# The eight transposes of the attention's q move from the PSUM tags s and o to the PSUM tag c

## The chip, the cores and the metric

One core of one Trainium2 chip runs the kernel. The time is device microseconds of one execution. The kernel before took 844.49 us, the median of three runs (843.57 to 844.58 us). The core has five engines with a queue of instructions each: TensorE (PE in the profile, with its weight loads as PEld), VectorE (DVE), ScalarE (ACT), GpSimd (POOL) and SyncE (SP). Matrix products are written into PSUM, which the kernel uses as eight banks of 128 x 512 float32.

## The reference, cut to what matters

One layer of an encoder on 512 tokens of width 1024. Three sub-layers follow one another, each between two RMS norms and added to the residual: a token mixer, a cross-attention into 256 memory rows, and a gated MLP with a short convolution. The change lies in the mixer, whose input projection feeds two groups of heads:

```python
h = rmsnorm(x, pre_mix_g)
aq, ak, av, hq, hf_fwd, hf_bwd, hi, hg = split_columns(h @ w_in, IN_SPLITS)
aq = rmsnorm(aq.reshape(b, n, 8, 64), q_norm_g)
ak = rmsnorm(ak.reshape(b, n, 2, 64), k_norm_g)
att = axial_gqa_attention(apply_rope(aq, cos, sin), apply_rope(ak, cos, sin), av)
rec = hgrn2_group(hq, hf_fwd, hf_bwd, hi, hg, ...)      # four recurrent heads
mixed = concatenate([att, rec]) @ w_out
```

So q has 8 heads of 64 columns for 512 tokens. It is projected token by token, normalised and rotated, and then transposed, since the scores need q with its columns on the partitions.

## The kernel before, in words

**Precision.** A float32 product is made of three matmuls on a high and a low part (`mm3`, lines 149 to 151). A value is split into these parts by a cast on ACT (line 103) and a subtraction on DVE (line 104).

**PSUM.** A tile of a bank is taken with `bank(tag)`. There are four tags, b, s, o and c, with two banks each. Tag b serves the projections whose output has its columns on the partitions, s and o the projections in token order and later the scores (s) and the transposed probabilities and outputs (o) of the attention. Tag c serves the recurrent cores (`hgrn_core`), and `spread_r` once at the start.

**Order.** The program is written as generators that `weave` interleaves in the text of the program. The framework then places the instructions on each engine's queue ahead of the run: an earlier place in the program goes first among those that it holds ready, and a later one may be put ahead of an earlier one that still waits. Once placed, the order in a queue is fixed. A tile whose tag has no free buffer waits for the release of an older one.

**The stage of the change.** `mix_projections` (line 662) ends with the projection of q in token order and the three projections of the last recurrent head:

- `proj_tm` on line 670 computes q for four blocks of 128 tokens. Its four banks are `tm_tags`, s, s, o, o: blocks 0 and 1 stand in the two banks of s, blocks 2 and 3 in the two of o. What is to be done with a block (`put_qn`, line 629) is only noted in the list `late`.
- `hgrn_in(3, late)` on line 671 projects head 3's q and its two forget gates (called f0 and f1 below) into tag b, each followed by a `scaled` use (line 451, DVE) that reads the bank, then by sigmoids on ACT (lines 470, 477, 478) and products on DVE (471, 480). After the first projection it runs `put_qn` of blocks 0 and 1, after the second that of blocks 2 and 3.
- `put_qn` of a block calls `norm_rope`, which reads the block's bank three times: a square on ACT (line 593) and two products on DVE (602 and 605). With the sums (595), the inverse root on POOL (167, 168, 597), the addition (606) and the scaling (607) it makes the rotated rows, which are split (103, 104) into `qs`. Then two groups of four transposes (line 637) each fill one bank: the first four heads, copied by ACT into `qT[0]` (line 641), and the last four, copied by DVE into `qT[1]` (line 639). There are 32 transposes and eight copies in all.
- After that comes one weave of three streams: the recurrent core of head 3 (`hgrn_core(3)`, tag c, whose first product is line 506 and its copy line 507), the attention (line 704: scores on line 711 in tag s, softmax from line 689, transposes of the probabilities on line 721 in tag o, and the weighing of v on line 733), and a filler (line 769): projections of the memory (`proj_fm` with 256 columns, two banks of tag b in turn, called memory column blocks below), whose output is split by `put_kx` (lines 103 and 104 on `ps_b`), then the output projection of the mixer.

The scores of item i take one bank of s and read `qT` at token block i % 4 of head i // 4. The high and low parts of scores are two matmuls.

Of the kernel before, what the change touches and what calls it, by code (L numbers as in the profile page):

```python
# [73 lines left out]
def layer(tc, io, out):  # L74
# [15 lines left out]
    def bank(tag):  # L90
        return ps.tile([P, 512], F32, name="ps_" + tag, tag=tag)
# [7 lines left out]
    def tmp4(shape, dt=F32):  # L99
        return t4.tile(shape, dt, name="tmp4", tag="tmp4")  # L100

    def split(hi, lo, src, eng=None):
        nc.scalar.copy(hi, src)  # L103
        (eng or nc.vector).tensor_sub(lo, src, hi.bitcast(F32))  # L104
# [48 lines left out]
    def blk(b):  # L153
        return slice(b * P, (b + 1) * P)
# [434 lines left out]
    def norm_rope(z, nh, which, b):  # L589
        n = nh * 64  # L590
        rope = qkv["rope"]
        u = tmp2()
        nc.scalar.activation(u[:, :n], z, ACT.Square, scale=r[:, b:b + 1])
        ss = small()
        nc.vector.tensor_reduce(ss[:, :nh], u[:, :n].rearrange("p (h d) -> p h d", h=nh), axis=AX.X, op=ALU.add)
        rz = rstd_of(ss[:, :nh], nh, 64)
        nc.gpsimd.tensor_scalar(rz[:, :nh], rz[:, :nh], r[:, b:b + 1], 0.0, op0=ALU.mult, op1=ALU.add)
        xn = tmp2()
        x3 = xn[:, :n].rearrange("p (h d) -> p h d", h=nh)
        st = rope[:, 2 * which + 1, b, :]  # L600
        ss4 = st.rearrange("p (i two) -> p i two", two=2)[:, None].to_broadcast([P, nh, 32, 2])
        nc.vector.tensor_tensor(out=u[:, :n].rearrange("p (h i two) -> p h i two", h=nh, two=2),
                                in0=pat(z, 1, [[64, nh], [2, 32], [-1, 2]]), in1=ss4, op=ALU.mult)
        ct = rope[:, 2 * which, b, :][:, None, :].to_broadcast([P, nh, 64])
        nc.vector.tensor_tensor(out=x3, in0=z.rearrange("p (h d) -> p h d", h=nh), in1=ct, op=ALU.mult)
        nc.vector.tensor_add(xn[:, :n], xn[:, :n], u[:, :n])
        nc.vector.tensor_tensor(out=x3, in0=x3, in1=rz[:, :nh, None].to_broadcast([P, nh, 64]), op=ALU.mult)
        return x3
# [20 lines left out]
    def put_qn(b, z):  # L629
        qr = norm_rope(z, 8, 0, b)  # L630
        qs = tmp4([P, 8, 2, 64], F32R)
        split(qs[:, :, 0, :], qs[:, :, 1, :], qr)
        q3 = qs.rearrange("p h a d -> p h (a d)")
        for g in range(2):
            o = bank("so"[g]).rearrange("p (k n) -> p k n", k=4)
            for i in range(4):
                nc.tensor.transpose(o[:, i, :].bitcast(F32R), q3[:, 4 * g + i, :], ident_r)
            if g:
                nc.vector.tensor_copy(qkv["qT"][g][:, :, blk(b)], o)
            else:  # L640
                nc.scalar.copy(qkv["qT"][g][:, :, blk(b)], o)
# [20 lines left out]
    def mix_projections():  # L662
        yield from proj_tm(hT, tm_tags, put_sg)
        mem_norm()
        yield from hgrn_in(1)
        yield from hgrn_in(2)
        mem_turn()
        yield from proj_tm(hT, tm_tags, put_kv, 256)
        late = []
        yield from proj_tm(hT, tm_tags, lambda b, z: late.append(lambda: put_qn(b, z)))  # L670
        yield from hgrn_in(3, late)
# [351 lines left out]
```

## Time and profile before

| | |
|---|---|
| median of three runs | 844.49 us (843.57 to 844.58) |
| the profiled execution's own time | 846.16 us |
| its span in the trace | 844.3 us |
| PE busy in the span | 828.5 us (98%) |
| DVE busy | 488.2 us (58%) |
| ACT busy | 427.7 us (51%) |
| mean granted clock of PE | 0.996 |

The span runs from the first to the last instruction that the trace shows; the profiled execution is 1.86 us longer than it. PE is busy nearly all the time, so a change of this size has to be read from the short stretch in which it works: 186 to 218 us after the start of the span. In the timelines of the prediction each row has the start in us, the duration in us, the engine, the line and operation, the tile written and the tiles read, their shape, how many instructions were merged, and in brackets the idle time of the engine before it with what ended that. In the table of stretches, each engine has its busy time with its count of instructions, then come the granted clock of PE, the share of time that the DMA engines were busy, and GB/s.

### The profile page before, as it was taken

What the parts mean: (1) busy time and instruction counts of PE and PEld (TensorE: products, weight loads), DVE (VectorE), ACT (ScalarE), POOL (GpSimd) and SP (SyncE); (2) the same over time, 40 slices, a digit from 0 to 9 for tenths busy, and PEclk for the clock granted to TensorE, in tenths of its full rate; (3) what the DMA queues carried; (4) which work ended last, traced back from release to release, by engine and by line L of the source; (5) the groups of instructions that cost most, each with busy time, mean ns of one, the idle gap of its engine ahead of it and who ended that gap; (6) DMA issues with size and microseconds to landing.
All of it is one profiled execution on the core that took longest, in us unless ns stands there. A gap on an engine that the chain in (4) does not pass through costs nothing.

```text
span 844.3 us, 11078 instructions
## 1 busy us (share of the span) xinstructions
PE 828.5 (98%) x4304; PEld 703.4 (83%) x4304; DVE 488.2 (58%) x759; ACT 427.7 (51%) x736; POOL 102.4 (12%) x163
## 2 busy tenths in 40 slices
PE   9999999997999999999999999999999999999996
PEld 7888888886999888888888998888888888888885
DVE  5364677619996775854444865555555557722224
ACT  6576656546898874645443553333333335511121
POOL 0212202317223201300001300000000000000001
PEclk9999999999999999999999999999999999999999
DMA  9687754477477643341302333322222222322312
GB/s 322 182 202 203 159 112 113 101 153 181 98 157 162 149 131 119 101 160 65 125 25 75 99 126 101 101 95 88 93 99 99 100 101 94 101 88 94 99 50 100
DMA packets 29796, 101.81 MB, mean 121 GB/s; under 512 B 3952, under 2 KB 4464, under 8 KB 29744
## 3 DMA queue, kind: packets, MB, share of 16 engines
q1 hardware_dynamic: 22752, 77.38, 27.3%
q0 software_dynamic: 6272, 22.81, 14.7%
q10 hardware_dynamic: 720, 0.92, 0.3%
q8 instruction: 34, 0.56, 0.3%
q14 instruction: 18, 0.15, 0.1%
HBM read 99.00 MB, written 2.10 MB: 120 GB/s over the span
## 4 chain that ended last, share of the span: by engine, by line
PE 91%; DVE 3%; ACT 2%; DMA 2%; POOL 1%; issue 1%; POOLq 0%; DVEq 0%; ACTq 0%
PE ps_b L149 9%; PE ps_b L150 9%; PE ps_b L151 9%; PE ps_s L151 6%; PE ps_s L149 6%; PE ps_s L150 6%; PE ps_o L149 6%; PE ps_o L151 6%; PE ps_o L150 6%; PE ps_c L149 4%; PE ps_c L150 4%; PE ps_c L151 4%; PE ps_c L516 3%; PE ps_o L733 2%; PE ps_s L711 2%; PE ps_o L721 2%
## 5 line engine op out<-in xcount | busy, mean ns | idle before, releaser
L104 DVE TENSOR_TENSOR wl<-raw,wh 128x1024 fp32r<-128x1024 f32 x93 | 113.8, 1224 | 199.9 <-ACT wh L103 199.8
L103 ACT CAST wh<-raw 128x1024 fp32r<-128x1024 f32 x93 | 97.9, 1053 | 206.2 <-PE ps_o L151 71.4
L149 PE MATMUL ps_b<-big,wh 128*128 128x512 f32 (+1 forms) x320 | 118.6, 371 | 2.1 <-DVE tmp L451 2.1
L150 PE MATMUL ps_b<-big,wh 128*128 128x512 f32 (+1 forms) x320 | 117.5, 367 | 0.0
L151 PE MATMUL ps_b<-big,wl 128*128 128x512 f32 (+1 forms) x320 | 117.3, 367 | 0.0
L149 PEld LDWEIGHTS ps_b<-big,wh 128*128 128x128 f32 x320 | 61.0, 191 | 11.3 <-DVE tmp L451 2.3
L151 PEld LDWEIGHTS ps_b<-big,wl 128*128 128x128 f32 x320 | 60.9, 190 | 9.3
L150 PEld LDWEIGHTS ps_b<-big,wh 128*128 128x128 f32 x320 | 60.9, 190 | 9.0
L177 POOL TENSOR_SCALAR small<-small 128x1 f32<-128x1 f32 x40 | 13.9, 348 | 440.7 <-ACT tmp L208 421.8
L149 PE MATMUL ps_s<-wh,big 128*128 128x512 f32 (+1 forms) x140 | 54.1, 387 | 0.0
L151 PE MATMUL ps_s<-wh,big 128*128 128x512 f32 (+1 forms) x140 | 53.3, 381 | 0.0
L150 PE MATMUL ps_s<-wl,big 128*128 128x512 f32 (+1 forms) x140 | 53.0, 379 | 0.0
L542 DVE TENSOR_TENSOR big<-big 128x512 f32<-128x512 f32 x64 | 47.9, 755 | 8.4 <-PE ps_c L516 4.6
L126 ACT CAST wh<-raw 128x1024 fp32r<-128x1024 f32 x35 | 36.7, 1048 | 30.3 <-PE ps_o L151 16.1
L149 PE MATMUL ps_o<-wh,big 128*128 128x512 f32 (+1 forms) x124 | 47.9, 386 | 0.0
L151 PE MATMUL ps_o<-wh,big 128*128 128x512 f32 (+1 forms) x124 | 46.7, 377 | 0.0
L150 PE MATMUL ps_o<-wl,big 128*128 128x512 f32 (+1 forms) x124 | 46.7, 377 | 0.0
L131 POOL DMA_DIRECT2D wl<-in_w_dram x35 | 31.2, 892 | 112.9 <-ACT wl L128 103.3
L104 DVE TENSOR_TENSOR big<-ps_o,big 128x512 fp32r<-128x512 f32 x52 | 35.7, 688 | 15.1 <-ACT big L103 14.9
L103 ACT CAST big<-ps_o 128x512 fp32r<-128x512 f32 x52 | 30.3, 586 | 19.6 <-PE ps_o L830 7.5
L149 PE MATMUL ps_b<-wh,big 128*128 128x512 f32 x92 | 36.7, 399 | 0.0
L150 PE MATMUL ps_b<-wl,big 128*128 128x512 f32 x92 | 36.2, 393 | 0.0
(248 smaller groups left out, 1949.2 us busy)
## 6 DMA issues: line engine op xcount, KB each, us to landing
raw<-in_w_dram SPq DMA_DIRECT2D x131, 512.0 KB, 3.3
wl<-in_w_dram POOLq DMA_DIRECT2D x35, 512.0 KB, 5.6
big<-in_x_dram SPq DMA_DIRECT2D x8, 512.0 KB, 7.5
big<-in_xt_dram SPq DMA_DIRECT2D x3, 512.0 KB, 7.8
big<-in_mem_dram POOLq DMA_DIRECT2D x2, 512.0 KB, 8.2
out_dram<-big SPq DMA_DIRECT2D x4, 256.0 KB, 2.0
out_dram<-big ACTq DMA_DIRECT2D x3, 256.0 KB, 2.0
big<-in_xt_dram SPq DMA_DIRECT2D x2, 256.0 KB, 3.5
```

Of the source, the lines that this page charges most:

```text
L103: nc.scalar.copy(hi, src)
L104: (eng or nc.vector).tensor_sub(lo, src, hi.bitcast(F32))
L126: nc.scalar.copy(wh, raw)
L131: nc.gpsimd.dma_start(wl, io["w"][i], accum_op=ALU.add)
L149: nc.tensor.matmul(o, a[0], b[0], start=start, stop=False)
L150: nc.tensor.matmul(o, a[0], b[1], start=False, stop=False)
L151: last_mm[0] = nc.tensor.matmul(o, a[1], b[0], start=False, stop=stop).ins
L516: nc.tensor.matmul(o[:, b, :], kc[:, blk(b)], pat(qk, b * P, [[2 * m, P // (2 * m)], [T + m, 2], [1, m]]), start=True, stop=True)
L542: nc.vector.tensor_tensor(out=c, in0=c, in1=pat(tt, toff + off, [[2, npair], [gap, 2], [0, m]]), op=ALU.mult)
L711: nc.tensor.matmul(s, qT[h // 4][:, h % 4, blk(qb)], kT[:, 2 * (h // 4) + c, :], start=c == 0, stop=c == 1)
L721: nc.tensor.transpose(o[:, c, :], e[:, 0, blk(c)], ident)
L733: nc.tensor.matmul(o, vv[:, c, h // 4].rearrange("p a d -> p (a d)"), pt[:, j, c, :], start=c + j == 0, stop=c == 3 and j == 1)
```

## The change

Both groups of transposes of a block take their bank from tag c, where the first took one from s and the second one from o. Nothing else in the program's text differs; the copies, the shapes and the order of the text are as before.

```diff
@@ -632,7 +632,7 @@
         split(qs[:, :, 0, :], qs[:, :, 1, :], qr)
         q3 = qs.rearrange("p h a d -> p h (a d)")
         for g in range(2):
-            o = bank("so"[g]).rearrange("p (k n) -> p k n", k=4)
+            o = bank("c").rearrange("p (k n) -> p k n", k=4)
             for i in range(4):
                 nc.tensor.transpose(o[:, i, :].bitcast(F32R), q3[:, 4 * g + i, :], ident_r)
             if g:
```

## The prediction, as put on record

> **What bounds the kernel now.** I read the busy shares first, then what PE waited for, then the stage of the change in a table of stretches, and last the timelines of the engines there.
>
> ```profile
> span 844.3 us, 11078 instructions
> PE 828.5 (98%) x4304; PEld 703.4 (83%) x4304; DVE 488.2 (58%) x759; ACT 427.7 (51%) x736; POOL 102.4 (12%) x163
> ```
>
> PE is idle for 844.3 - 828.5 = 15.8 us in all. A change that adds and removes no work can gain only there, or by the clock. PE's waits, as line waiting, releaser, total us, times, longest:
>
> ```profile
> PE ps_s L637 <- DVE tmp L104: 2.5, 2, 1.9
> PE ps_b L149 <- DVE tmp L451: 2.1, 1, 2.1
> ```
>
> These are PE's two longest waits and both belong to the stage of q: 4.6 us together. Neither is released by the end of a read of another block's bank. The transposes wait for the split of their own rows (104), the first memory column block that is not yet done waits for the read of f1 (451).
>
> ```profile
> 200.00:203.60 3.60, 3.58 (x31) 3.38 (x31) 3.56 (x6) 3.46 (x6) 3.19 (x4) 1.00 0.98 224
> 203.60:208.50 4.90, 0.89 (x10) 0.75 (x9) 4.90 (x9) 2.27 (x5) 4.11 (x6) 1.00 0.92 181
> 208.50:212.00 3.50, 3.50 (x17) 3.50 (x18) 2.88 (x5) 3.09 (x5) 0.00 (x0) 0.54 0.96 214
> 215.00:260.00 45.00, 44.55 (x346) 42.06 (x345) 42.10 (x91) 39.82 (x81) 12.15 (x12) 1.00 0.66 141
> ```
>
> From 203.6 to 208.5 us PE works 0.89 us of 4.90, and DVE all 4.90: DVE's row of work sets the end of this hole. The hole has a sequel: the granted clock is 0.54 in the next 3.5 us, which costs 3.5 x 0.46 = 1.6 us. From 215 to 260 us PE is busy again (idle 0.45 us).
>
> ```profile
> 196.05 0.46 PE L637 MATMUL ps_s<-ident_r,tmp 128*128 128x128 f32 x4
> 200.02 0.54 PE L637 MATMUL ps_s<-ident_r,tmp 128*128 128x128 f32 x4 [0.58 <-DVE tmp L104]
> 200.71 0.46 PE L637 MATMUL ps_o<-ident_r,tmp 128*128 128x128 f32 x4
> 203.33 0.28 PE L151 MATMUL ps_b<-big,wl 128*128 128x256 f32 x1
> 205.50 0.54 PE L637 MATMUL ps_s<-ident_r,tmp 128*128 128x128 f32 x4 [1.89 <-DVE tmp L104]
> 208.50 0.38 PE L149 MATMUL ps_b<-big,wh 128*128 128x256 f32 x1 [2.12 <-DVE tmp L451]
> 211.66 0.41 PE L149 MATMUL ps_b<-big,wh 128*128 128x256 f32 x1
> 211.88 0.97 PE L506 MATMUL ps_c<-tmp,tmp 128*128 128x128 f32 x6
> 212.61 0.54 PE L637 MATMUL ps_s<-ident_r,tmp 128*128 128x128 f32 x4
> 213.32 0.46 PE L506 MATMUL ps_c<-tmp,tmp 128*128 128x128 f32 x2
> 213.53 1.17 PE L711 MATMUL ps_s<-big 128*128 128x512 f32 x4
> 215.99 0.28 PE L151 MATMUL ps_b<-big,wl 128*128 128x256 f32 x1
> 217.18 0.28 PE L149 MATMUL ps_b<-big,wh 128*128 128x256 f32 x1
> ...
> 238.92 0.46 PE ps_s L711 x2
> 239.38 0.44 PE ps_o L721 x4
> ```
>
> (The last two rows are from the chain of waits: start, time, tile, line.) The rows at 196.05, 200.02, 205.50 and 212.61 are the first groups of blocks 0 to 3. Block 0's second group comes only at 200.71, 4.7 us after its first. That is the wait that the change removes.
>
> ```profile
> 193.87 0.68 DVE L605 TENSOR_TENSOR tmp<-ps_s,big 128x512 f32<-128x512 f32 x1
> 199.88 0.68 DVE L605 TENSOR_TENSOR tmp<-ps_o,big 128x512 f32<-128x512 f32 x1
> 201.21 0.68 DVE L639 CAST big<-ps_o 128x512 fp32r<-128x512 f32 x1
> 204.77 0.68 DVE L104 TENSOR_TENSOR tmp<-tmp,tmp 128x512 fp32r<-128x512 f32 x1
> 207.76 0.68 DVE L451 TENSOR_TENSOR tmp<-ps_b,big 128x512 f32<-128x512 f32 x1
> 209.66 0.75 DVE L502 SCALAR_TENSOR_TENSOR tmp<-big,oml,tmp 128x512 f32<-128x512 f32 x1 [0.62 <-ACT big L478]
> ```
>
> The read of block 2 ends at 199.88 + 0.68 = 200.56; block 0's second group follows at 200.71. So the shared bank is real. But PE had other work until then, and the copy at 201.21 has no waiter.
>
> ```profile
> 196.54 0.60 ACT L641 CAST big<-ps_s 128x512 fp32r<-128x512 f32 x1
> 200.60 0.59 ACT L641 CAST big<-ps_s 128x512 fp32r<-128x512 f32 x1
> 210.76 0.83 ACT L513 COPY tmp<-big 128x512 f32<-128x512 f32 x1
> 213.18 0.59 ACT L641 CAST big<-ps_s 128x512 fp32r<-128x512 f32 x1 [1.59 <-PE ps_s L637]
> 213.81 0.59 ACT L507 COPY big<-ps_c 128x512 f32<-128x512 f32 x1
> 214.30 0.38 ACT L103 CAST big<-ps_b 128x256 fp32r<-128x256 f32 x1
> 215.27 1.28 ACT L692 ACT_TABLE_LOAD   x1
> 216.57 0.69 ACT L692 ACTIVATE tmp<-ps_s,small 128x512 f32<-128x512 f32 x1
> 217.16 0.19 ACT L692 ACTIVATION_READ_ACCUMULATOR tmp<-ps_s,small 128x1 f32 x1
> ```
>
> Scores 0 need only `qT[0]` of block 0, copied by 196.54 + 0.60 = 197.14, and k, which an earlier stage made. A bank of s stood empty from 197.14 to 205.50. Yet scores 0 start at 213.53, behind block 3's transposes, while the memory column block of a later place in the program was let in ahead of them (its last matmul is at 203.33). I infer that the banks of a tag are given out in the order of the program: scores 0 can't have one before block 3's first group has taken its own. The row at 214.30 fits: the split of that memory column block needs a big tile behind the core's, and goes right after line 507 has taken that.
>
> **The change part by part.** Thirty-two transposes and eight copies stay, with their shapes and engines. No DMA, no weight and no arithmetic is touched. Only the banks differ.
>
> (1) **Block 0's second group** may follow its first, at 196.3 instead of 200.71. On PE it is 0.3 us of work in a stretch without idle time either way: 0. Its copy, 0.68 us of DVE, moves ahead of 201.21. DVE does the same set of work before the read of f1 at 207.76, so that moves by nothing on balance; by one copy, 0.7 us, either way if a copy lands on the other side of it. I take 0.
>
> (2) **Scores 0 and 1** are freed. In s they are now next behind blocks 0 and 1 of q, whose reads end by 193.87 + 0.68 = 194.55. They are ready at 197.14 and at 200.60 + 0.59 = 201.19, and stand ahead of the memory column block in the program, so PE should take them before 203.6. Two items are 2 x 0.46 = 0.92 us of PE's work (row at 238.92). That memory block slides back into the idle 0.58 and 1.89 us, and the end of the hole at 208.50 stays. Behind it 0.92 us are gone: -0.92. The bounds are 0 (they are not hoisted) and -0.92 - 0.46 - 0.88 = -2.3, if scores 2 and the eight transposes of the first two probabilities (0.44 us for four, row at 239.38) come into the hole too. I take -0.92, because the softmax needs DVE, which is full until 208.4.
>
> (3) **The clock.** The hole shrinks from 4.9 to about 4.0 us. Rows bound the effect: a wait of 0.58 us at 200.02 left the clock at 1.00 in its stretch, the hole of 4.9 us was followed by 0.54. So it is 0 to -1.6 us; 4.0 is nearer to 4.9, and I take 0.
>
> The Trainium skill ("TensorE: Matmul & The Clock Gate", Part 1) says the clock falls to half after an idle window of about 3.4 us that runs free of the kernel, and (Part 4) that transposes don't count as busy in the same way. By that rule the hole of 4.0 us still can hold such a window, which speaks against a gain here, and the sum would be the same; the stretch at 0.54 after 4.9 us with only transposes in it agrees.
>
> (4) **The core of head 3** takes its first bank of c behind all eight groups. Now its product of line 506 (211.88, ready when line 502 ends, 209.66 + 0.75 = 210.41) goes ahead of block 3's transposes (212.61). With two banks it will have to wait for the copy of block 3's first group: transposes, then 0.59 us of line 641, then 506. Behind 506 are queued the copy 507, the split at 214.30 and with it the next memory column block. PE's cover is the rest of the memory column block in hand (24 matmuls, 16 of them done by 211.88), at 0.12 us each (215.99 to 217.18, eleven matmuls, ten steps) to 0.21 us (208.50 to 211.66, sixteen, fifteen steps), 1 to 1.7 us against some 0.9 us from the transposes to the end of the copy. I take 0; without the cover it is +0.9. The upper bound is in the rivals.
>
> (5) **From 214 us on** PE is full and works through the same amounts, so what is gained stays, up to the 0.45 us of idle time there: 0.
>
> Sum: -0.92 us. On the profiled execution 846.16 - 0.92 = 845.2, on its span 843.4. That execution is 1.67 us above the median; on the median, 844.49 - 0.92 = **843.6 us**.
>
> **The rivals.**
>
> **A, the forecast:** the scores move and nothing else does, 843.6, own range 842.6 to 844.4.
>
> **B, more of the hole is filled, or the clock holds:** -0.92 - 1.6 = -2.5, so 842.0; with all of (2) and (3), -3.9, 840.6. For it: the hole is the only one of its size, and scores 1 may fall into its middle and divide it. Against: DVE's row from 187 on has no room for the softmax, and 4.0 us is still long.
>
> **C, no effect:** the planner puts the scores no earlier, for a reason other than the order of banks. 844.5. For it: they are PE work of a later stage. Against: the rows of (2).
>
> **D, slower, by the two banks of c:** ACT has a gap of 1.59 us before block 3's copy at 213.18. With scores 0 ready early, their exponential is put into that gap: table load 1.28, exponential 0.69, 0.19 to read the sum, 2.2 us from 211.59 (210.76 + 0.83) to 213.8. Block 3's copy then ends at 214.4, and only then may line 506 start, 2.5 us later than now. PE's cover ends near 212.9 to 213.5, so some 0.9 to 1.5 us are idle, and the next memory block, which hangs on 507 and the split, comes 2.5 us later with 0.7 us uncovered: +1.6 to +2.2, less 0.92, and another 1.6 if the clock falls again: +0.7 to +2.9, with +2.0 for the middle, 846.5. It decides from the point at which the copy ends more than PE's 1 to 1.7 us of cover behind the transposes. For it: the planner fills gaps greedily, as the table shows. Against: the maximum of scores 0 must be reduced on DVE first, which is full until 208.4.
>
> **How the numbers follow.** A 0.40, B 0.28, C 0.07, D 0.25. About 0.2% (1.7 us, 842.8 to 846.2) is what a measurement here can tell from no change. Faster: B and a tenth for A's tail, 0.38. Same: A's body, C and a little of D, 0.32. Slower: D and, in A, the chance that a queue shifted at 196 us brings new waits in the 100 us behind it, 0.30. The range goes from B with nearly all its terms, 840.5, to D at its bound and a half us for such waits, 848.0.
>
> **What would show it.** Right: L637 writes only `ps_c`, block 0's two groups adjacent near 196; L711 first before 203; PE idle from 199 to 208.5 down from 4.6 to 3.7 us; L451 still near 207.8; clock near 0.54 behind it. B: clock 1.00 after 208. D: a table load before block 3's L641, and L506 near 214 behind an idle PE. Wrong outright: L451 of f1 moves by over 1 us, or new waits of PE appear after 215.

## The result, and the profile after

The changed kernel takes **843.18 us** (median of 20 runs, 842.38 to 844.77) against 844.84 us of the kernel before on the same chip (20 runs, 843.55 to 846.86): a ratio of 0.998, with an interval of 0.9973 to 0.9986. The time lies 0.4 us from the forecast of 843.6 us, the gain is 1.66 us against a forecast of 0.92. The profiled execution took 842.82 us.

The page after has the same instructions on PE, and 1.3 us less of PE's busy time (828.5 before):

```profile
span 841.0 us, 11080 instructions
PE 827.2 (98%) x4304; PEld 702.0 (83%) x4304; DVE 488.7 (58%) x759; ACT 427.0 (51%) x736; POOL 102.4 (12%) x163
```

The two profiled executions can't be laid on each other by the time of the span, since the stage is reached 1.94 us earlier in this one with the same queues ahead of it. Below, **T0** is the start of block 0's first transposes (196.05 before, 194.11 after), and "after T0" counts from there. The fence holds the first matmuls of line 830, a stage far behind, before and then after (first and last start in us):

```profile
L830 PE MATMUL ps_o<-ident,tmp x8: 272/272/273, 392.3 to 394.5; 128*128 128x128 f32 x8
```

```profile
L830 PE MATMUL ps_o<-ident,tmp x8: 272/272/273, 389.0 to 391.2; 128*128 128x128 f32 x8
```

From T0 that is 392.3 - 196.05 = 196.25 us before and 389.0 - 194.11 = 194.89 us after: 1.36 us are won behind T0, the rest of the 3.3 us between the two spans was there before the change begins.

PE's waits after, in the stretch from 193 to 256 us (in all, times, longest):

```profile
PE ps_b L149 <- DVE tmp L451: 2.3, 1, 2.3
PE ps_c L637 <- DVE tmp L104: 0.6, 1, 0.6
PE ps_o L733 <- DVE big L104: 0.5, 1, 0.5
PE ps_o L721 <- ACT tmp L697: 0.4, 1, 0.4
```

The sum is 3.8 us. Before, it was the two rows of the prediction and the same 0.5 us at line 733: 5.1 us. The wait of 1.89 us for block 2's split is gone, and one of 0.4 us at the probabilities is new. PE's timeline, after:

```profile
194.11 0.79 PE L637 MATMUL ps_c<-ident_r,tmp 128*128 128x128 f32 x8
...
197.10 0.39 PE L711 MATMUL ps_s<-big 128*128 128x512 f32 x1
198.05 0.85 PE L637 MATMUL ps_c<-ident_r,tmp 128*128 128x128 f32 x8 [0.56 <-DVE tmp L104]
198.74 0.46 PE L711 MATMUL ps_s<-big 128*128 128x512 f32 x1
...
201.20 0.63 PE L711 MATMUL ps_s<-big 128*128 128x512 f32 x2
...
204.85 0.39 PE L149 MATMUL ps_b<-big,wh 128*128 128x256 f32 x1 [2.33 <-DVE tmp L451]
...
205.54 0.85 PE L637 MATMUL ps_c<-ident_r,tmp 128*128 128x128 f32 x8
...
206.66 0.41 PE L151 MATMUL ps_b<-big,wl 128*128 128x256 f32 x1
...
210.06 0.63 PE L711 MATMUL ps_s<-big 128*128 128x512 f32 x2
210.63 0.85 PE L637 MATMUL ps_c<-ident_r,tmp 128*128 128x128 f32 x8
211.86 0.65 PE L721 MATMUL ps_o<-ident,tmp 128*128 128x128 f32 x4 [0.38 <-ACT tmp L697]
212.35 1.14 PE L506 MATMUL ps_c<-tmp,tmp 128*128 128x128 f32 x8
```

Block 0's two groups are one row of eight. Scores 0 and 1 (two matmuls each) run before 203. The idle stretch ends at 204.85, which is 10.74 us after T0; before, it ended at 208.50, 12.45 us after T0. Block 2's transposes, which before lay inside the idle stretch, now follow it at 205.54. The core's first product (506) starts 18.2 us after T0, where it was 15.8.

The same stretch on DVE, and on ACT, after:

```profile
203.52 0.68 DVE L605 TENSOR_TENSOR tmp<-ps_o,big 128x512 f32<-128x512 f32 x1
204.12 0.68 DVE L451 TENSOR_TENSOR tmp<-ps_b,big 128x512 f32<-128x512 f32 x1
204.72 0.68 DVE L104 TENSOR_TENSOR tmp<-tmp,tmp 128x512 fp32r<-128x512 f32 x1
205.32 0.68 DVE L606 TENSOR_TENSOR tmp<-tmp,tmp 128x512 f32<-128x512 f32 x1
```

```profile
195.08 0.64 ACT L477 ACTIVATE big<-tmp 128x512 f32<-128x512 f32 x1
...
207.18 1.28 ACT L692 ACT_TABLE_LOAD   x1
...
211.71 0.57 ACT L641 CAST big<-ps_c 128x512 fp32r<-128x512 f32 x1
```

The read of f1 (451) comes 10.01 us after T0, before 11.71. Block 2's split (104), block 3's addition (606) and block 2's copy (639) stood ahead of it and now stand behind it: three pieces of 0.6 us. And the first sigmoid of the gate f0 (477) runs 1.0 us after T0. Before it ran at

```profile
201.08 0.63 ACT L477 ACTIVATE big<-tmp 128x512 f32<-128x512 f32 x1
```

5.0 us after T0. The prediction had not looked at that row.

The stretches after (PE, PEld, DVE, ACT, POOL busy; granted clock; DMA share; GB/s):

```profile
203.60:208.50 4.90, 3.65 (x25) 3.64 (x26) 4.90 (x10) 4.05 (x7) 4.29 (x4) 0.81 0.82 207
208.50:212.00 3.50, 3.12 (x20) 2.64 (x19) 3.44 (x7) 3.50 (x8) 0.00 (x0) 0.78 0.88 137
```

The low clock costs 4.9 x 0.19 + 3.5 x 0.22 = 1.7 us in this execution, as it did in the profiled one before (1.6). So the clock doesn't make the difference between these two executions. For the medians this doesn't follow: over all runs whose clock is on record, the mean granted clock of the whole span is 0.997 in the changed kernel (0.995 to 0.999, 32 runs) and 0.994 in the kernel before (0.993 to 0.996, 97 runs). What that may be worth is taken up at step (3) and in the last section.

### The profile page after: what moved, and what is told of

Same layout as the page of the kernel before. It is cut to its first block, busy times and chain, and to the rows that moved or that the text cites. A ratio compares the mean times of both kernels' runs of the same rounds, so it can differ in the third digit from the quotient of the medians.

```text
span 841.0 us, 11080 instructions
## 1 busy us (share of the span) xinstructions
PE 827.2 (98%) x4304; PEld 702.0 (83%) x4304; DVE 488.7 (58%) x759; ACT 427.0 (51%) x736; POOL 102.4 (12%) x163
## 4 chain that ended last, share of the span: by engine, by line
PE 92%; ACT 3%; DVE 2%; POOL 1%; DMA 1%; issue 1%; POOLq 0%; DVEq 0%; ACTq 0%
PE ps_b L149 9%; PE ps_b L150 9%; PE ps_b L151 9%; PE ps_s L151 6%; PE ps_s L149 6%; PE ps_s L150 6%; PE ps_o L149 6%; PE ps_o L151 6%; PE ps_o L150 6%; PE ps_c L151 4%; PE ps_c L149 4%; PE ps_c L150 4%; PE ps_c L516 3%; PE ps_o L733 2%; PE ps_o L721 2%; PE ps_s L711 1%
```

## The experiments

The question is which of three things pays: the scores in the idle stretch, the gates that are no longer held up, or the earlier read of f1. Differences of medians are against the kernel before on the same chip.

### One group alone to c

Against the kernel before, each kernel changes one word: `bank("co"[g])` sends the first groups to c and leaves the second ones in o, `bank("sc"[g])` does the reverse.

```diff
-            o = bank("so"[g]).rearrange("p (k n) -> p k n", k=4)
+            o = bank("co"[g]).rearrange("p (k n) -> p k n", k=4)
```

> Only the first group of each block goes to c, the second stays in o, so s is freed and the wait for block 2's bank stays. Theory S (the gain is the scores' matmuls that fill PE's hole, as predicted): scores 0 and 1 start before 203 us, the read of f1 (line 451) stays near 207.8, PE idles 3.7 us in the stage, and the kernel takes 0.9 us less than before, most of the change's gain. Theory G (the gain comes from the gates: the held-back copy into qT[1] was the first write of its big tile, and head 3's gate tiles, next in that pool, had to wait for it; with the bank free they are made 4 us earlier and the read of f1 moves up by 1.7 us): line 477 stays near 201, nothing is gained from the hole's end, and at most half of the gain of 1.7 us is seen.

```diff
-            o = bank("so"[g]).rearrange("p (k n) -> p k n", k=4)
+            o = bank("sc"[g]).rearrange("p (k n) -> p k n", k=4)
```

> Only the second group of each block goes to c; the first stays in s, so the scores stay behind block 3. Theory S: nothing is gained, time within 0.3 us of before, since scores 0 start near 213 as before. Theory G: line 477 of f0 runs near 197 in place of 201, the read of f1 ends near 206 to 207 in place of 208.4, the idle time of PE in the stage falls from 4.6 us to about 3, and 0.8 to 1.7 us are gained.

With the first groups in c: 844.54 us, a ratio of 1.0003 (0.9991 to 1.0014). With the second: 844.35 us, 1.0 (0.9991 to 1.0009). Neither half alone gains. PE's waits with the first groups in c, in the stretch from 193 to 256 us:

```profile
PE ps_b L149 <- DVE tmp L451: 2.1, 1, 2.1
PE ps_c L637 <- DVE tmp L104: 1.6, 2, 0.9
PE ps_o L733 <- DVE big L104: 0.7, 1, 0.7
PE ps_o L721 <- ACT tmp L697: 0.6, 1, 0.6
PE ps_c L516 <- ACT tmp L513: 0.3, 1, 0.3
```

The scores do what the forecast priced. The two waits of the transposes fall from 2.5 to 1.6 us, by the 0.9 us of scores 0 and 1, and the read of f1 stays where it was, 206.13 - 194.42 = 11.71 us after T0. But 0.2, 0.6 and 0.3 us come back at lines 733, 721 and 516 within the next stretch, and the sum is 5.3 us. PE's later work was taken early, and ACT and DVE could not follow. So the scores by themselves show no gain.

With the second groups in c the scores stay late, but the first sigmoid of f0 comes at 194.15, 1.0 us after its T0 of 193.18. The waits of the transposes are 3.8 us in this kernel, 0.5 us at line 733 is as before, and 0.5 and 0.3 us are new behind them: 5.1 us, nothing won.

### What the bank held up: a first write made early

In the kernel before, block 0's second group and its copy are the first write of `qT[1]`. The guess: the buffers of the large tiles are given out in the order of the program too, so that head 3's gate tiles, which come later in the program, must wait for that write. If so, it is a wait of the planning ahead of the run: on the chip the sigmoid starts at 201.08, just before the copy at 201.21, so only its place in ACT's queue is late. A write of one column on POOL, which block 0's copy overwrites, takes the wait away and leaves all banks as they were.

```diff
-        qr = norm_rope(z, 8, 0, b)
+        b or nc.gpsimd.memset(qkv["qT"][1][:, 0, 0:1].bitcast(F32), 0.0); qr = norm_rope(z, 8, 0, b)
```

> The kernel before with its banks s and o, and one more instruction: POOL writes one column of qT[1] before block 0 is normalised, so that this big tile is taken early; the copies overwrite it. It takes away only what theory G says the late bank held up. Theory G: line 477 of f0 near 197 though block 0's second group still comes behind the read of block 2 (200.7), and 0.5 to 1.7 us gained. If the late bank itself, or the scores, made the gain: line 477 stays near 201 and the time is that of before within 0.3 us.

It took 843.26 us, a ratio of 0.9988 (0.9979 to 0.9996). Its first sigmoid on ACT, and the end of the idle stretch on PE:

```profile
194.55 0.64 ACT L477 ACTIVATE big<-tmp 128x512 f32<-128x512 f32 x1
```

```profile
204.61 0.75 PE L637 MATMUL ps_s<-ident_r,tmp 128*128 128x128 f32 x4 [3.46 <-DVE tmp L104]
```

T0 is 193.57 here. The sigmoid is back at 1.0 us after T0, as the guess about the buffers says: one column is enough. PE resumes 11.04 us after T0, and waits 4.0 us in all. By the medians, most of the change's gain is had without a single bank moved, and without the earlier read of f1, which comes 11.5 us after T0 here.

The same write with the first groups in c:

```diff
-            o = bank("so"[g]).rearrange("p (k n) -> p k n", k=4)
+            o = bank("co"[g]).rearrange("p (k n) -> p k n", k=4)
```

> The first groups in c and the early touch of qT[1] together; the second groups stay in o, so block 0's second group still waits for the read of block 2. If the change's gain is the two effects together (scores freed, gates early) and the late second group itself costs nothing: about the changed kernel's time, 1.0 to 1.7 us below before. If the gain hangs on where f1's read lands in DVE's order (theory H): here it comes behind block 2's split, so the hole ends no more than 0.6 us earlier than before and under 0.8 us is gained.

It took 845.27 us, 1.0005 (0.9997 to 1.0014). Early gates and early scores together do not make the gain:

```profile
PE ps_b L149 <- DVE tmp L451: 2.2, 1, 2.2
PE ps_c L637 <- DVE tmp L104: 1.2, 3, 0.7
PE ps_o L721 <- ACT tmp L697: 0.7, 1, 0.7
...
PE ps_o L721 <- DVE big L104: 0.2, 1, 0.2
```

The idle stretch is 3.1 us (0.68, 0.25 and 2.17), nearly as short as in the changed kernel, and 2.2 us of waits follow it (the rows left out are 0.7 us at line 733 and 0.3 at 516). Sum 5.3 us. What the changed kernel has and this one lacks is the order on DVE: here the split of block 2 still stands ahead of the read of f1 (204.80 - 193.67 = 11.13 us after T0). But the idle stretch is only 0.2 us longer than in the changed kernel; most of what is missing lies in the waits behind it (2.2 us against 0.9), and that these come of the order is not shown.

### The order on DVE alone

Now the banks are as before, and only the split and the transposes of blocks 2 and 3 are put behind the third projection, so that the read of f1 is ahead of them in the program.

```diff
...
-        qr = norm_rope(z, 8, 0, b)
-        qs = tmp4([P, 8, 2, 64], F32R)
+        if z is not None and b > 1: turned.append(norm_rope(z, 8, 0, b)); return
+        qr = turned.pop(0) if z is None else norm_rope(z, 8, 0, b); qs = tmp4([P, 8, 2, 64], F32R)
...
-        yield from hgrn_in(3, late)
+        yield from hgrn_in(3, late); put_qn(2, None); put_qn(3, None)
```

> The kernel before with its banks s and o; the split and the transposes of blocks 2 and 3 are put behind the third projection's use in the program, so that DVE reads f1 right behind the products of block 3, as in the changed kernel. Theory H: the first matmuls behind the hole start some 10.7 us after block 0's transposes (12.45 in the kernel before), PE idles 1.5 us less, 1 to 2 us are gained without any bank moved. If the order of f1's read doesn't matter: within 0.5 us of before.

It took 843.51 us, 0.9988 (0.9979 to 0.9997). PE's waits:

```profile
PE ps_b L149 <- DVE tmp L451: 3.1, 1, 3.1
PE ps_s L637 <- DVE tmp L104: 0.6, 1, 0.6
...
```

The read of f1 comes 203.61 - 193.68 = 9.93 us after T0, as in the changed kernel, with no score and no sigmoid (5.0 us after T0) early. 1.2 us are won, with 4.2 us of waits (0.5 of them at line 733).

The same edit in the changed kernel (the lines of `put_qn`, edited as above, are left out):

```diff
...
-        yield from hgrn_in(3, late)
+        yield from hgrn_in(3, late); put_qn(2, None); put_qn(3, None)
```

> The changed kernel with the same shift of the split and transposes of blocks 2 and 3 behind the third projection. f1 is read at the same place as in the changed kernel, so theory H expects its hole unchanged and a time within 0.8 us of the changed kernel's, 842.4 to 844. If the transposes of block 2, now behind sixteen matmuls of the memory block, delay what hangs on them, it is slower by the new wait.

It took 844.72 us, 1.0 (0.9991 to 1.0009). The idle stretch is that of the changed kernel to 0.01 us, and the gain is gone:

```profile
PE ps_b L149 <- DVE tmp L451: 2.3, 1, 2.3
PE ps_c L637 <- DVE tmp L104: 0.7, 2, 0.6
...
PE ps_o L721 <- ACT tmp L697: 0.5, 1, 0.5
PE ps_c L506 <- ACT big L641: 0.5, 1, 0.5
PE ps_s L711 <- ACT tmp L692: 0.3, 1, 0.3
```

This is what tells a theory of the idle stretch alone from a count of all waits: 2.9 us of idle stretch in both kernels, but 4.9 us of waits here (0.6 of them at line 733, left out) and 3.8 there. The wait of 0.5 us at line 506 for block 3's copy (641) is the one that the prediction's rival D described.

Both edits that gained without a moved bank, the early column and the later text, in one kernel:

> The kernel before (banks s and o), with both of the others' edits: the split and transposes of q's blocks 2 and 3 behind the third gate projection, and one column of head 3's first q written early. Alone they gave 843.51 us (4.2 us of waits from T0 on) and 843.26 us (4.0 us). Theory 1 (the time follows the waits of PE, and the stretch without matmuls ends when DVE comes to f1's read, which stands at the same place of DVE's order, behind L605 of block 3, whether head 3's gates are early or not): L477 of f0 falls from 5.0 to 1.0 us after T0, f1's read stays 9.5 to 10.5 us after T0, the waits stay near 4 us, and the time is 843.2 to 843.6 us. Theory 2 (early gates and an early read of f1 are two gains that add): f1's read near 8 us after T0, waits near 3 us, 842.2 us.

It took 843.37 us, 0.9982 (0.9972 to 0.9993). The gains don't add, as its first theory said. The read of f1 stays (204.8 - 194.63 = 10.2 us after T0); PE waits 3.4 us for it and 4.5 us in all. DVE's order sets that read, and early gates give DVE nothing less to do ahead of it.

### The read of f1 moved to either side, in the changed kernel

To ask only for an earlier read, one `put_qn` in place of two runs after each gate's projection, which puts block 3 behind f1.

```diff
-            for job in between[:2]:
+            for job in between[:2 if put is put_q else 1]:
...
-            between = between[2:]
+            between = between[2 if put is put_q else 1:]
```

> The changed kernel, with block 3 of q normalised after the third projection of head 3 and not before, so that DVE reads f1 some five operations, 3 us, earlier. No arithmetic is different. If the end of the hole is set by DVE's order ahead of the read of f1, as both theories say, the hole of 2.3 us in the changed kernel closes, the low clock behind it goes with it (1.6 us), and the kernel takes 2 to 4 us less than the changed one: 839 to 841 us. If it is then block 3's transposes and the core of head 3 behind them (two banks of c) that bound, a new wait of PE of 1 us or more stands before line 506 or 721 and the gain is under 1 us.

It took 846.57 us, 1.0022 (1.0012 to 1.0032). On DVE and on PE:

```profile
202.92 0.68 DVE L451 TENSOR_TENSOR tmp<-ps_b,big 128x512 f32<-128x512 f32 x1
...
211.65 0.68 DVE L689 TENSOR_REDUCE small<-ps_s 128x1 f32<-128x512 f32 x1
```

```profile
214.53 1.22 PE L711 MATMUL ps_s<-big 128*128 128x512 f32 x2 [5.72 <-ACT tmp L692]
```

The read is 6.2 us after T0 (196.75), and the idle stretch in front of it is gone. But scores 0 and 1 hold the two banks of s until the softmax has read them, DVE takes the maximum (689) of the first only at 211.65, and PE stops for 5.72 us at scores 2. The stall was not removed but moved to the next tag.

The reverse keeps the changed kernel's banks and issues the read of f1 behind block 2's split:

```diff
...
-            nc.vector.tensor_mul(z, o, r_bc)
+            with tc.issue_after(held.pop()) if held else ExitStack(): nc.vector.tensor_mul(z, o, r_bc)
...
-        split(qs[:, :, 0, :], qs[:, :, 1, :], qr)
+        nc.scalar.copy(qs[:, :, 0, :], qr); ins = nc.vector.tensor_sub(qs[:, :, 1, :], qr, qs[:, :, 0, :].bitcast(F32)).ins; b == 2 and held.append(ins)
```

> The changed kernel with one order forced: the read of f1 (line 451) is issued on DVE only behind the split of block 2's rows, as in the kernel before. Theory H (the gain is the earlier end of PE's hole: f1 is read 10.0 us after block 0's transposes in place of 11.7, and that order came with the gates; scores in the hole alone give back what they gain): f1 is read three DVE operations, 1.8 us, later, PE idles some 1.5 us more, and the time is that of before within 0.8 us, 844 to 845. If the freed banks make the gain whatever the order of f1: it stays 1.2 us or more below before.

It took 846.05 us, 1.0017 (1.0008 to 1.0026), with the read 207.11 - 195.28 = 11.83 us after T0. The gain is gone, but the run changes more than was asked: with the gate late, ACT takes the first exponential ahead of its sigmoid and loads its table twice more.

```profile
206.06 1.28 ACT L692 ACT_TABLE_LOAD   x1 [0.89 <-DVE small L689]
...
208.63 1.28 ACT L477 ACT_TABLE_LOAD   x1
...
213.46 1.28 ACT L692 ACT_TABLE_LOAD   x1
```

So it agrees with the late read as the cause and doesn't show it alone.

### The core's place behind block 3

In the changed kernel block 3's groups go to o, which frees the core (506) from them.

```diff
-            o = bank("c").rearrange("p (k n) -> p k n", k=4)
+            o = bank("o" if b == NB - 1 else "c").rearrange("p (k n) -> p k n", k=4)
```

> The changed kernel, with block 3's two groups of transposes in o; blocks 0 to 2 stay in c. In the program's order the first matmuls of head 3's core (L506) then stand ahead of block 3's transposes, as they did before the change. Theory 1 (the time follows the waits of PE from T0 to 60 us on, of which the changed kernel has 3.8 us, and 0.38 of them come from the core of head 3 standing behind block 3 in c): the stretch without matmuls stays 2.9 us, L506 comes some 16 us after T0 instead of 18.2, the wait of L721 for ACT L697 goes, and the time is 842.8 us, 0.4 under the changed kernel. Theory 2 (the place of that core decides nothing, other work fills in): 843.2 us, waits as in the changed kernel. Theory 3 (o now has block 3's transposes between the turns of the scores, and they are late): a new wait of PE at L721 or L711 behind block 3 of 0.85 us or more, 844 us.

> The changed kernel itself beside the other two on one chip, as their measure. If its gain belongs to the kernel and not to one chip, its ratio to the kernel before is 0.998 again, 843.0 to 843.4 us, with a stretch of 2.9 us without matmuls and some 3.8 us of waits from T0 on; if it belongs to the chip, its ratio is 0.999 or more.

Block 3 in o took 842.62 us, 0.9973 (0.9961 to 0.9985); the changed kernel again, on the same chip, 843.16 us, 0.998 (0.9967 to 0.9992), so its gain goes with the kernel and not with one chip. PE's waits with block 3 in o:

```profile
PE ps_b L149 <- DVE tmp L451: 2.3, 1, 2.3
PE ps_b L149 <- DVE big L104: 0.6, 1, 0.6
...
```

The wait at line 721 is gone and the core starts 210.60 - 194.41 = 16.2 us after T0 in place of 18.2, as expected. But a wait of 0.6 us appears at the next memory column block, and the sum, with 0.6 at line 637 and 0.2 at 733, is 3.7 us. The median is the lowest of all kernels here, 0.54 us under the changed one, but the two intervals overlap: that it is faster than the changed kernel is not shown.

### All kernels side by side

| kernel | read of f1 after T0 | PE's waits, 193 to 256 us | mean granted clock, all runs | median less that of before |
|---|---|---|---|---|
| before | 11.7 | 5.1 | 0.9944 | |
| changed | 10.0 | 3.8 | 0.9972 | -1.66 |
| changed, again | 10.0 | 3.4 | 0.9975 | -1.31 |
| block 3 in o | 10.0 | 3.7 | 0.9963 | -1.85 |
| early column | 11.5 | 4.0 | 0.9948 | -1.44 |
| later text, s and o | 9.9 | 4.2 | 0.9956 | -1.20 |
| later text and early column | 10.2 | 4.5 | 0.9960 | -1.10 |
| later text, c | 10.0 | 4.9 | 0.9969 | 0.0 |
| second groups in c | 11.1 | 5.1 | 0.9955 | -0.35 |
| first groups in c | 11.7 | 5.3 | 0.9956 | -0.16 |
| first groups in c, early column | 11.1 | 5.3 | 0.9959 | +0.56 |
| read of f1 held | 11.8 | 5.8 | 0.9953 | +1.34 |
| block 3 behind f1 | 6.2 | 7.0 | 0.9940 | +1.87 |

The waits are those of one profiled execution each (two of the changed kernel give 3.8 and 3.4 us), the medians of 11 to 20 runs; the clock of the kernel before is the mean of its 97 runs beside these kernels. The count of waits less 5.1 gives the change of the median to about 0.6 us in every row; the read of f1 alone does not (the last row, and the 10.0 us that go with 0.0). Nor does the clock: the early column gains 1.44 us at nearly the clock of before, and the later text in c gains nothing at 0.9969.

## Why the prediction was right, and where it was not

**The time** came out near the forecast, but the sum had two steps that failed against each other. That it came so near is in part luck: the scores of step (2) by themselves show no gain, and what came in its place was put at 0 in steps (1) and (3).

**Step (1), block 0's second group at 0, failed**, and with it the statement that the read of f1 "moves by nothing on balance". It moved by 1.7 us (11.7 to 10.0 us after T0), which the prediction itself named as "wrong outright". The shared bank was indeed nothing to PE, as the step said. What was overlooked is what hung on the copy behind it: the first write of `qT[1]`, and behind that, by the order in which buffers are given out, the tiles of head 3's gates. The early column shows that the write sets the place of the gates' sigmoid (5.0 to 1.0 us after T0); the rule of the buffers is the inferred reason. The prediction had inferred this very rule for the banks of s and for the split at 214.30, and didn't ask it of the copy at 201.21, of which it says that it "has no waiter". With the gates' work early, and block 0's and 1's transposes in c, the read of f1 stands ahead of block 2's split on DVE. That this order is worth about 1.2 us (0.3 to 1.8 by the interval) without any moved bank is shown by the later text, though a part of it may be the clock's (0.9956 against 0.9944); why exactly the two groups in c together lead to it, and neither alone, lies in the planning ahead of the run and stays open.

**Step (2), the scores at -0.92, was right in place and size.** They run at 197.10, 198.74 and 201.20, and with the first groups in c they fill 0.9 us of the waits. The idle stretch then adds up: it was 4.6 us, the scores alone leave 3.7 (first groups in c), the order on DVE alone leaves 3.7 (later text, s and o), and both together leave the 2.9 us of the changed kernel, where the prediction had 3.7. **Step (5), that what is gained stays, failed**: in that kernel it all came back behind the idle stretch. The prediction's 0.45 us of idle time in the full stretch was that of the kernel before; taking work early from a stretch that is full makes it less so. In the changed kernel only 0.4 us came back.

**Step (3), the clock at 0, fits the two profiled executions and not all runs.** The cost was 1.7 us after and 1.6 before, though spread over two stretches at 0.81 and 0.78 where the prediction's sign was 0.54. But the mean clock of all runs is 0.997 against 0.994. Sorted by clock, runs at 0.995 or 0.996 took 843.18 us in the changed kernel (median of 12) and 843.91 in the kernel before (40): 0.7 us, against 1.4 between all of them (843.17 and 844.56). This is a sorting of runs and not an experiment; how much of the gain is the clock's stays open, and it may be half.

**Step (4), the core behind block 3 at 0, and rival D.** D's mechanism came about nearly as written: the table load at 207.18 precedes block 3's copy at 211.71, and line 506 came 2.4 us later after T0 (2.5 in the text). But its price was 0.4 us of wait and not 1.6 to 2.2, because scores 2 at 210.06 and the memory block covered PE meanwhile. With a little less cover, in the kernel with the later text and c, 0.5 us of wait stand at line 506, among 1.1 us of further waits with which the gain is lost.

**Rivals B and C.** The scores did move, so C did not occur. The half of B in which the clock holds came about in some runs: 11 of the 32 have a mean clock of 0.999, and a stretch of 3.41 us at half clock, the shortest seen in this stage, would leave no more than 1 - 0.5 x 3.41 / 841 = 0.998. None of the 97 runs before lies above 0.996. But those 11 runs took 842.66 us by their median, against 843.20 of the other 21, and not 842.0 or less.

## What to carry to other kernels

A wait for a bank costs more than its own engine shows: follow the instruction that it delays to the buffer that it writes first, and ask which later tiles are given out behind that one. A score or product taken early into an idle stretch is only lent, if the engines that must use it are full; what counts is the sum of the bottleneck engine's waits until it runs full again, and beside it the granted clock of all runs and not of the profiled one alone. Experiments that do one part at a time show which part keeps its gain. Where the gain comes from an order that a planner happened to choose, a small further edit can lose all of it (844.72 us here) or move the stall to the next tag (846.57 us).

## What the hardware showed

The clock fell after a gap that was short, and not at the same place in two executions of the same queues. In the second profile of the changed kernel, on PE:

```profile
204.58 0.58 PE L149 MATMUL ps_b<-big,wh 128*128 128x256 f32 x1 [2.34 <-DVE tmp L451]
...
210.75 0.41 PE L151 MATMUL ps_b<-big,wl 128*128 128x256 f32 x1
```

Here the matmuls take 0.41 us, in place of the 0.28 us seen at full clock, as soon as the gap of 2.34 us ends, and keep doing so until 211. In the first profile the gap was 2.33 us, and the first matmul of 0.41 us came 1.8 us behind its end, at 206.66; the clock was back near 210. The second profile's rows for the stretches shown above for the first:

```profile
203.60:208.50 4.90, 3.92 (x21) 3.92 (x22) 4.20 (x8) 3.93 (x7) 4.01 (x4) 0.56 0.76 201
208.50:212.00 3.50, 3.50 (x22) 3.36 (x22) 3.50 (x8) 3.28 (x8) 0.00 (x0) 0.64 0.95 150
```

At half clock that is (4.9 x 0.44 + 3.5 x 0.36) / 0.5 = 6.8 us here, and by the same sum 3.4 us in the first profile. The clock's records in the traces know only these two lengths in this stage, 3.41 us (eight of the 13 profiled executions, the kernel before among them) and 6.83 us (five). The second 3.41 us cost about 1 us here: line 830 starts 194.9 and 195.5 us after T0 in the two profiles, 0.6 us later in the second, though PE waits 0.4 us less. That is as much as most differences between the kernels here. In the early column's profile, one of the five, line 830 comes 196.2 us after T0, no earlier than before the change, so its gain shows in its medians and its waits alone.

The Trainium skill ("TensorE: Matmul & The Clock Gate", Part 1) says that the clock halves after an idle window of about 3.4 us that runs free of the kernel. That the place varies, and that the low stretches are one or two times 3.41 us long, agrees with such a window; that a gap of 2.3 us is enough does not. In the 3.41 us before the clock fell PE was busy for 1.79 us in the first profile and 1.43 us in the second. No threshold follows from this: before the change, the 3.41 us from 201.94 held 1.67 us of PE's work, and no fall came right behind them.
